# A projection moved to the token choice, and gathered rows evicted four at a time

## The chip, the cores and the metric

The kernel runs on one NeuronCore of a Trainium2 chip. Its time is the device time of one execution in microseconds (us). Five engines work side by side, each on its own list of instructions: PE (matmuls; PEld is its weight load), DVE and ACT (elementwise work), POOL (elementwise work on SBUF) and SP, which issues the DMA transfers here. A transfer is issued in the order of SP's list; an instruction that waits for a semaphore holds up what stands behind it on its engine.

## The reference

Two transformer blocks run one after the other on 512 tokens of width 1024, in float32. The first has a recurrent mixer, a cross attention and a dense feed-forward layer. The second has windowed attention beside a gated linear attention, then an expert layer and a gated embedding. The change is in the second block's end:

```python
h = h + merged @ w_out[l]
h = h + expert_choice_ffn(rmsnorm_2(h, norm_ffn[l]), w_router[l], w_exp_gate[l], w_exp_up[l], w_exp_down[l])
ple_gate = jax.nn.sigmoid(rmsnorm_2(h, norm_ple[l]) @ w_ple_gate[l])
h = h + ple_gate * (p[l] @ w_ple[l])
```

In `expert_choice_ffn` each of 16 experts takes the 64 tokens with the highest affinity to it, computes `silu(x @ gate) * (x @ up) @ down` with its own three 1024x1024 matrices, and adds the result, times the affinity, to those tokens. `p` is an input of 512 x 256 and `w_ple` one of 256 x 1024; their product depends on nothing else.

## The kernel before

**Precision.** Dense products run as three matmuls (`mm3`, L124 to L126) on operands that are split into a rounded part `hi` (ACT, L103) and a rest `lo` (DVE, L104). Expert products run in plain float32. In the trace such a float32 matmul, of an expert or of a gather, shows as two records.

**Output projection and router.** `proj_out` computes `merged @ w_out` in two halves of 512 columns; L88 loads the weights, and between the weights' split and the second half's matmuls it calls `more`, which loads expert weights. Behind each tile of the second half, `router` transposes the tile (L1263), multiplies it with the router's weights (L1269), takes the norm's factor on POOL (L188), makes a softmax and transposes the affinities on PE (L1292).

**Token choice.** DVE finds the 64 largest affinities of each expert in eight rounds (L1313, L1314), marks and numbers them (L1315, L1317). PE transposes the marks (L1323).

**Experts.** They go in eight groups g of two experts. `gather` builds a 0/1 matrix on DVE, and `rows(k)` (k = 0 to 7) picks the tokens with four matmuls into a quarter of a PSUM tile `pout`, of which there are two; ACT evicts each quarter with a scale (L1387). `hidden(e)` runs gate and up (L1478, 32 matmuls), `down(e)` the third matrix (L1503, 16 matmuls), `turned` transposes (L1493), `scatter` adds a group's result to x (L1518, L1519). In one group PE does: the first expert's hidden, the previous expert's down, the second's hidden with eight scatters, the first's down, then the gather for the next group. PE's order here is written out by hand.

**Expert weights.** The 48 matrices come as 96 pieces of 2 MB, in the order in which PE uses them: pieces 0 to 3 are expert 0's gate and up, then come, for each expert, its gate and up (4) and the previous one's down (2). So group g from 1 on uses the twelve pieces from 10 + 12(g-1). They land in a ring of eight places of 16 KB per partition: `wnext` (6), opened before the output projection, and `wlast` (2), opened when its memory is free. Pieces 6, 7 and 8 go to other tiles at first: `act_hi`, the place that `pp` gets later, and four `y4` tiles. `used` frees places and issues the next loads; a load waits until PE has finished with the piece that had the place.

**p's projection** is part of the expert loop. From group 1's end to group 2 the ring leaves three places free (`kept`). In group 2 these take p, w_ple and the split operands; in group 3 PE transposes p (L204) and multiplies (L124 to L126) into `pp`. After the experts, `pp` is multiplied with the gate.

Of the kernel before, what the change touches and what calls it, by code (L numbers as in the profile page):

```python
# [10 lines left out]
F32 = mybir.dt.float32  # L11
# [8 lines left out]
P = 128  # L20
# [15 lines left out]
def two_blocks_kernel(ctx: ExitStack, tc: tile.TileContext, A: dict, out: bass.AP, stage: int = 99):  # L36
# [751 lines left out]
    WNEXT, WLAST = 6, 2  # L788
# [38 lines left out]
    kept = [0]  # L827
# [17 lines left out]
    def used(e, m):  # L845

        free([name for _, name in pieces.pop((e, m))[::4] if name])
        load(max(0, sum(room.values()) - kept[0]))
# [6 lines left out]
    with ExitStack() as blk:  # L855
# [439 lines left out]
        side.close()  # L1295
        open_ring(late, "wnext", WNEXT, side="right")
        load(3)

        def more():
            load(WNEXT - 3)  # L1300

# [3 lines left out]
        if stage == 6:  # L1305
            return store_and_stop(x)

# [25 lines left out]
    with ExitStack() as blk:  # L1333
# [18 lines left out]
        def projected():  # L1352
            return pool.tile([P, NT, D], F32, name="pp", tag="pp", bufs=1)

        w = projected()
        homes[WNEXT + 1] = w
        homes[WNEXT + 2] = [y4() for _ in range(4)]
        load(3 + WLAST)
# [3 lines left out]
        def gather(g):  # L1362
# [17 lines left out]
            def rows(k):  # L1380
# [3 lines left out]
                for t in range(NT):  # L1384
                    PE.matmul(ps[0][:, j * P:(j + 1) * P], src[:, t, k * P:(k + 1) * P], sel[:, t, :],  # L1385
                              start=(t == 0), stop=(t == NT - 1))
                S.activation(xg[:, :, k, :], ps[0][:, j * P:(j + 1) * P].rearrange("p (e s) -> p e s", e=2), AF.Copy,  # L1387
                             scale=gcol[:, k:k + 1])
# [19 lines left out]

        def load_p():
            pr = w8((NT, 256))  # L1410
            nc.sync.dma_start(pr, A["p_2"][0, 0].rearrange("(t p) c -> p t c", p=P))
            raw = w8()
            nc.sync.dma_start(raw, A["w_ple_2"][0].rearrange("(k p) c -> p k c", p=P))
            hi, lo, pT = w8(dt=F32R), w8(dt=F32R), w8((2, 2, T), F32R)
            w8()
            return pr, raw, hi, lo, pT

        def split8(raw, hi, lo):
            S.copy(hi, raw)
            V.tensor_sub(lo, raw, hi.bitcast(F32))  # L1420
            return hi, lo

        def split_p(pr, raw, hi, lo, pT):
            split8(raw, hi, lo)
            for t in range(NT):
                transpose_split(lambda k0, n: (pT[:, 0, :, t * P:(t + 1) * P], pT[:, 1, :, t * P:(t + 1) * P]),
                                pr[:, t, :], 2)

        def project_p(pr, raw, hi, lo, pT):
            wh, wl = hi, lo  # L1430
            pp = projected()
            for t in range(NT):
# [102 lines left out]
        with tc.manual_schedule(engines={mybir.EngineType.PE}):  # L1535
            gT = None
            for g in range(NE // 2):
                a, b = 2 * g, 2 * g + 1
                if g:
# [3 lines left out]
                    if a == 6:  # L1543
                        split_p(*praw)
# [196 lines left out]
```

## Time and profile before

| | us |
|---|---|
| median of 3 runs (1952.05 to 1952.69) | 1952.14 |
| the profiled execution | 1952.34 |
| its span, first to last instruction | 1950.6 |
| PE busy | 1870.0 (96%) |
| DVE busy | 917.5 (47%) |
| ACT busy | 719.7 (37%) |
| POOL busy | 66.9 (3%) |

Of the span, the output projection ends at about 1362 us, the token choice at 1382, and the experts at about 1889. Times in the rows count from the span's start. PEclk is the granted clock of PE as a share of 2.4 GHz; 0.5 is 1.2 GHz. Durations of matmuls overlap, so what a matmul costs in a row of matmuls is read from one start to the next.

### The profile page before, as it was taken

The numbers are of one execution on the slowest core, as the hardware profiler recorded it, in microseconds if no ns is written. First come the engines' busy times: TensorE is split into PE (matmuls) and PEld (weight loads), VectorE is DVE, ScalarE is ACT, GpSimd is POOL, SyncE is SP. The second block draws the span as 40 slices with busy tenths as digits, with TensorE's granted clock in tenths as the row PEclk, the third lists the DMA queues.
The fourth block names the chain that finished last, engine by engine and source line by source line (L and its number), as shares of the span: only waits on it lengthen the run. The fifth ranks groups of instructions, "written<-read, shape, count | busy, mean of one in ns | idle before, by whom it ended". The sixth has DMA issues, their size and how long they took to land.

```text
span 1950.6 us, 24203 instructions
## 1 busy us (share of the span) xinstructions
PE 1870.0 (96%) x9723; PEld 1364.2 (70%) x9723; DVE 917.5 (47%) x1659; ACT 719.7 (37%) x1329; POOL 66.9 (3%) x103
## 2 busy tenths in 40 slices
PE   7999999999999999999999999999699989999998
PEld 6777788888888888887787778888344435434446
DVE  5777777465543444446875564453312221221146
ACT  4454774343342322325665454322121112111134
POOL 0000220000000000002000000000000000000000
PEclk9999999999999999999999999999799989999999
DMA  6222226431233333324222222336779977999951
GB/s 206 55 61 74 56 86 182 137 108 55 67 118 98 97 97 97 98 76 111 75 63 58 75 68 74 87 122 244 314 286 424 417 327 315 428 426 426 426 206 44
DMA packets 140050, 330.85 MB, mean 170 GB/s; under 512 B 9247, under 2 KB 88851, under 8 KB 127779
## 3 DMA queue, kind: packets, MB, share of 16 engines
q1 hardware_dynamic: 139522, 328.91, 46.4%
q8 instruction: 76, 1.25, 0.3%
q0 software_dynamic: 416, 0.41, 0.1%
q14 instruction: 36, 0.29, 0.0%
HBM read 327.19 MB, written 2.10 MB: 169 GB/s over the span
## 4 chain that ended last, share of the span: by engine, by line
PE 82%; DVE 7%; ACT 5%; issue 2%; DMA 1%; POOL 1%; SPq 0%; POOLq 0%; ACTq 0%; DVEq 0%
PE pd L125 16%; PE pd L124 16%; PE pd L126 16%; PE pd L1478 11%; PE pscore L1503 6%; PE pout L1385 4%; DVE lo L104 1%; ACT hi L103 1%; ACT xg L1387 1%; PE pout L1149 1%; PE pout L204 1%; POOL rs L188 1%; PE pscore L400 1%; PE pout L1046 1%; PE pscore L1119 1%
## 5 line engine op out<-in xcount | busy, mean ns | idle before, releaser
L104 DVE TENSOR_TENSOR lo<-raw,hi 128x1024 fp32r<-128x1024 f32 x208 | 253.5, 1221 | 329.5 <-ACT hi L103 326.6
L103 ACT CAST hi<-raw 128x1024 fp32r<-128x1024 f32 x208 | 218.1, 1049 | 419.6 <-PE pd L126 226.0
L124 PE MATMUL pd<-hi,act_hi 128*128 128x512 f32 (+2 forms) x584 | 227.9, 390 | 1.5 <-ACT act_hi L206 1.1
L125 PE MATMUL pd<-lo,act_hi 128*128 128x512 f32 (+2 forms) x584 | 226.6, 389 | 0.8 <-DVE lo L104 0.8
L124 PE MATMUL pd<-act_hi,hi 128*128 128x512 f32 (+1 forms) x592 | 224.2, 380 | 0.5 <-ACT act_hi L206 0.5
L126 PE MATMUL pd<-act_hi,lo 128*128 128x512 f32 (+1 forms) x592 | 224.5, 379 | 0.0
L125 PE MATMUL pd<-act_lo,hi 128*128 128x512 f32 (+1 forms) x592 | 224.2, 379 | 0.0
L1478 PE MATMUL pd<-w,xg 128*64 128x512 f32 x992 | 220.5, 600 | 0.0
L126 PE MATMUL pd<-hi,act_lo 128*128 128x512 f32 (+1 forms) x512 | 199.9, 391 | 0.0
L1478 PEld LDWEIGHTS pd<-w,xg 128*64 128x64 f32 x992 | 69.7, 138 | 135.6 <-issue 135.5
L124 PEld LDWEIGHTS pd<-hi,act_hi 128*128 128x128 f32 x584 | 110.2, 189 | 22.1 <-ACT act_hi L206 2.8
L124 PEld LDWEIGHTS pd<-act_hi,hi 128*128 128x128 f32 x592 | 111.1, 188 | 20.0 <-ACT act_hi L206 1.0
L126 PEld LDWEIGHTS pd<-act_hi,lo 128*128 128x128 f32 x592 | 111.5, 188 | 19.4 <-issue 0.2
L125 PEld LDWEIGHTS pd<-act_lo,hi 128*128 128x128 f32 x592 | 111.6, 188 | 19.1 <-DVE act_lo L207 0.4
L125 PEld LDWEIGHTS pd<-lo,act_hi 128*128 128x128 f32 x584 | 110.3, 189 | 20.2 <-DVE lo L104 1.3
L1503 PE MATMUL pscore<-w,m 128*64 128x512 f32 x496 | 109.6, 594 | 0.7 <-ACT m L1495 0.7
L126 PEld LDWEIGHTS pd<-hi,act_lo 128*128 128x128 f32 x512 | 96.6, 189 | 18.0 <-DVE act_lo L207 0.5
L253 DVE TENSOR_TENSOR x<-x,pd 128x512 f32<-128x512 f32 x83 | 55.2, 685 | 97.2 <-PE pd L126 55.9
L125 PE MATMUL pd<-lo,hh 128*128 128x512 f32 x256 | 99.7, 390 | 0.0
L124 PE MATMUL pd<-hi,hh 128*128 128x512 f32 x256 | 99.7, 389 | 0.0
L126 PE MATMUL pd<-hi,hl 128*128 128x512 f32 x256 | 99.6, 389 | 0.0
L188 POOL TENSOR_TENSOR rs<-ms,mhalf 128x1 f32<-128x1 f32 (+1 forms) x45 | 33.7, 750 | 1811.1 <-DVE ms L187 1806.9
(454 smaller groups left out, 2840.5 us busy)
## 6 DMA issues: line engine op xcount, KB each, us to landing
w<-in_w_exp_dram SPq DMA_DIRECT2D x93, 2048.0 KB, 14.0
raw<-in_w_in_dram SPq DMA_DIRECT2D x80, 512.0 KB, 3.7
raw<-in_w_up_dram SPq DMA_DIRECT2D x32, 512.0 KB, 4.2
raw<-in_w_down_dram SPq DMA_DIRECT2D x32, 512.0 KB, 3.6
raw<-in_w_xkv_dram SPq DMA_DIRECT2D x16, 512.0 KB, 5.1
raw<-in_w_out_dram SPq DMA_DIRECT2D x16, 512.0 KB, 3.8
x<-in_x_dram SPq DMA_DIRECT2D x8, 512.0 KB, 7.4
raw<-in_w_xq_dram SPq DMA_DIRECT2D x8, 512.0 KB, 3.9
```

Of the source, the lines that this page charges most:

```text
L103: S.copy(hi[:, :size], raw[:, :size])
L104: V.tensor_sub(lo[:, :size], raw[:, :size], hi[:, :size].bitcast(F32))
L124: PE.matmul(ps, ah, bh, start=first, stop=False)
L125: PE.matmul(ps, ah, bl, start=False, stop=False)
L126: PE.matmul(ps, al, bh, start=False, stop=last)
L188: G.tensor_tensor(rs[:, :n], ms[:, :n], mhalf[:, :n], op=OP.pow)
L204: PE.transpose(ps[:, k, :], src[:, (k0 + k) * P:(k0 + k + 1) * P], ident)
L253: return lambda t, ps: V.tensor_add(x[:, t, c:c + 512], x[:, t, c:c + 512], ps)
L400: PE.matmul(ps[H * hf:H * hf + H, t, :].rearrange("p (n two b) -> p two n b", two=2, b=B), km[:, o:o + H], qv, start=True, stop=True)
L1385: PE.matmul(ps[0][:, j * P:(j + 1) * P], src[:, t, k * P:(k + 1) * P], sel[:, t, :], start=(t == 0), stop=(t == NT - 1))
L1478: PE.matmul(ps[64 * half:64 * half + 64, :], xg[:, e % 2, k, :], w[:, 512 * half:512 * half + 512], start=(k == 0), stop=(k == KT - 1))
L1503: PE.matmul(py[64 * half:64 * half + 64, :], h[:, k % 4, 64 * (k // 4):64 * (k // 4) + 64], w[:, 512 * half:512 * half + 512], start=(k == ...
```

## The change

p's projection moves from the expert loop to the output projection and the token choice. `more` loads p and both halves of w_ple and transposes p; after `proj_out`, the second half of w_ple is split by ACT and POOL, and the 48 matmuls follow into a tile `pp` of its own. The ring keeps eight places, five in `wnext` and three in `wlast`, since `pp` takes one from the memory ahead; piece 5 goes to `act_hi` and 6 to the `y4` tiles, and no piece to `pp`'s place. The rule that kept three places free goes. In `rows`, DVE evicts four quarters at once.

```diff
-    WNEXT, WLAST = 6, 2
+    WNEXT, WLAST = 5, 3
...
-        load(max(0, sum(room.values()) - kept[0]))
+        load(sum(room.values()))
...
+        pp = late.enter_context(tc.tile_pool(name="pp", bufs=1, side="right")).tile([P, NT, D], F32, name="pp")
         open_ring(late, "wnext", WNEXT, side="right")
         load(3)
...
         def more():
+            pr = grow_tile().rearrange("p (t c) -> p t c", t=NT)
+            nc.sync.dma_start(pr, A["p_2"][0, 0].rearrange("(t p) c -> p t c", p=P))
+            wple.append(chunk_b(w_ple, 0, 0))
+            load_ahead(w_ple, 0, 512)
             load(WNEXT - 3)
+            for t in range(NT):
+                transpose_split(lambda k0, n: (pT[:, 0, :, t * P:(t + 1) * P], pT[:, 1, :, t * P:(t + 1) * P]),
+                                pr[:, t, :], 2)
...
+        raw = loaded.pop((w_ple.tensor.name, w_ple.offset, 0, 512))
+        hi, lo = [pools["w"].tile([P, WC], F32R, name=n) for n in ("hi", "lo")]
+        S.copy(hi, raw)
+        G.tensor_sub(lo, raw, hi.bitcast(F32))
+        wple.append([w.rearrange("p (a b) -> p a b", a=2) for w in (hi, lo)])
+        for n in range(2):
+            wh, wl = wple[n]
+            for t in range(NT):
+                ts = slice(t * P, (t + 1) * P)
+                ps = pd()
+                for k in range(2):
+                    mm3(ps, pT[:, 0, k, ts], pT[:, 1, k, ts], wh[:, k, :], wl[:, k, :], k == 0, k == 1)
+                S.copy(pp[:, t, 512 * n:512 * n + 512], ps)
...
-        homes[WNEXT + 1] = w
-        homes[WNEXT + 2] = [y4() for _ in range(4)]
-        load(3 + WLAST)
+        homes[WNEXT + 1] = [y4() for _ in range(4)]
+        load(2 + WLAST)
...
-                S.activation(xg[:, :, k, :], ps[0][:, j * P:(j + 1) * P].rearrange("p (e s) -> p e s", e=2), AF.Copy,
-                             scale=gcol[:, k:k + 1])
+                if j == 3:
+                    V.tensor_mul(xg[:, :, k - 3:k + 1, :].rearrange("p e k s -> p k e s"),
+                                 ps[0].rearrange("p (k e s) -> p k e s", k=4, e=2),
+                                 gcol[:, k - 3:k + 1, None, None].to_broadcast([P, 4, 2, CAP]))
...
-                    if a == 6:
-                        split_p(*praw)
...
-                if a == 4:
-                    kept[0] = 0
-                    praw = load_p()
-                    pheld = held[-3:]
...
-                if a == 6:
-                    pp = project_p(*praw)
-                    free(pheld)
...
-                if a == 2:
-                    kept[0] = 3
```

PE's list at the end of the output projection, before: the last tile's second half is transposed (L1263) and routed (L1269), the affinities are transposed (L1292), and the next row already belongs to the token choice.

```order
L126 MATMUL pd<-hi,u_10578 128x256
L1263 MATMUL pout<-ident,x 128x128 x4
L1269 MATMUL pscore<-wr,grow 128x16 x4
L1292 MATMUL pscore<-ident,aff 16x128
L1323 MATMUL pscore<-ident,raw 128x16 x8
L1385 MATMUL pout<-m_11194,x 128x128 x16
```

The same place now (`pT` is p transposed and split):

```order
L1262 MATMUL pout<-ident,x 128x128 x2
L124 MATMUL pd<-hi,pT 128x512
L125 MATMUL pd<-lo,pT 128x512
L1262 MATMUL pout<-ident,x 128x128 x2
L1268 MATMUL pscore<-wr,grow 128x16 x2
L126 MATMUL pd<-hi,pT 128x512
L124 MATMUL pd<-hi,pT 128x512
L125 MATMUL pd<-lo,pT 128x512
L126 MATMUL pd<-hi,pT 128x512
L1268 MATMUL pscore<-wr,grow 128x16 x2
L124 MATMUL pd<-hi,pT 128x512
L125 MATMUL pd<-lo,pT 128x512
```

The 48 matmuls of the projection stand between the router's last transpositions: 14 ahead of the last L1291 (L1292 before), the other 34 behind it and ahead of L1348 (L1323 before).

SP's list at the loads of pieces 6, 7 and 8, before, with the semaphores that each row waits for (`y` is a `y4` tile):

```order
L841 DMA act_hi<-in_w_exp_dram 128x4096 [waits DMAHW2_49,PE_49]
L841 DMA pp<-in_w_exp_dram 128x4096 [waits DMAHW3_49,DMAHW6_49,DVE_49,PE_49]
L839 DMA y_11177<-in_w_exp_dram 128x1024 [waits DMAHW4_49]
L839 DMA y_11178<-in_w_exp_dram 128x1024 [waits DMAHW5_49]
L839 DMA y_11179<-in_w_exp_dram 128x1024
L839 DMA y_11180<-in_w_exp_dram 128x1024 [waits DMAHW7_49]
```

The same place now, from piece 5 to piece 8:

```order
L840 DMA act_hi<-in_w_exp_dram 128x4096 [waits DMAHW4_49,PE_49]
L838 DMA y_11281<-in_w_exp_dram 128x1024 [waits DMAHW5_49,DMAHW2_49,Pool_49]
L838 DMA y_11282<-in_w_exp_dram 128x1024 [waits DVE_49,PE_49]
L838 DMA y_11283<-in_w_exp_dram 128x1024 [waits DMAHW7_49,PE_49]
L838 DMA y_11284<-in_w_exp_dram 128x1024 [waits DMAHW0_49]
L840 DMA w_11290<-in_w_exp_dram 128x4096 [waits DMAHW1_49]
L840 DMA w_11292<-in_w_exp_dram 128x4096 [waits DVE_49]
```

The `y4` tiles now lie where the split w_ple lies: the first quarter waits for POOL's subtraction, the second for a matmul of the projection's first half (n = 0), the third for the projection's last matmul. Pieces 7, 8 and 9 stand behind them.

## Rows read from the trace of the kernel before

**Rows 1.** The page: busy time of the engines, and the transfers' rate in the 40 slices.

```profile
PE 1870.0 (96%) x9723; PEld 1364.2 (70%) x9723; DVE 917.5 (47%) x1659; ACT 719.7 (37%) x1329; POOL 66.9 (3%) x103
...
GB/s 206 55 61 74 56 86 182 137 108 55 67 118 98 97 97 97 98 76 111 75 63 58 75 68 74 87 122 244 314 286 424 417 327 315 428 426 426 426 206 44
```

**Rows 2.** The waits of PE from 1340 us to the end: who waited for whom, us in total, times, longest.

```profile
PE pout L1385 <- ACT xg L1387: 22.0, 48, 0.5
PE pscore L1323 <- DVE raw L1315: 12.5, 1, 12.5
PE pout L204 <- DVE w L207: 5.2, 1, 5.2
```

**Rows 3.** PE's timeline of one gather, that for group 2, and the first expert behind it: start, us, engine, line, operation, out<-in, records, and the idle time before with its releaser.

```profile
1493.95 1.16 PE L1385 MATMUL pout<-oh,act_hi 128*128 128x128 f32 x8
1495.57 1.16 PE L1385 MATMUL pout<-oh,act_hi 128*128 128x128 f32 x8 [0.46 <-ACT xg L1387]
...
1498.80 2.05 PE L1385 MATMUL pout<-oh,act_hi 128*128 128x128 f32 x16 [0.46 <-ACT xg L1387]
1501.31 1.16 PE L1385 MATMUL pout<-oh,act_hi 128*128 128x128 f32 x8 [0.46 <-ACT xg L1387]
...
1505.54 0.96 PE L1393 MATMUL pscore<-aff,oh 128*128 128x16 f32 x8
...
1506.91 13.95 PE L1478 MATMUL pd<-w,xg 128*64 128x512 f32 x64
```

**Rows 4.** PE's timeline: the starts of the first expert of groups 1, 3 and 4 (that of group 2 is in rows 3).

```profile
1447.04 13.95 PE L1478 MATMUL pd<-w,xg 128*64 128x512 f32 x64
...
1566.79 13.95 PE L1478 MATMUL pd<-w,xg 128*64 128x512 f32 x64
...
1647.66 13.95 PE L1478 MATMUL pd<-w,xg 128*64 128x512 f32 x64
```

**Rows 5.** Stretches behind the first gather and in the expert stage: from:to, length, then busy us (and records) of PE, PEld, DVE, ACT and POOL, PE's clock, the transfers' share of 16 engines and GB/s.

```profile
1395.00:1400.00 5.00, 3.62 (x28) 3.05 (x27) 0.00 (x0) 1.10 (x3) 0.00 (x0) 1.00 0.85 305
...
1660.00:1860.00 200.00, 191.75 (x972) 85.83 (x970) 39.46 (x68) 30.28 (x67) 0.00 (x0) 1.00 1.01 427
```

**Rows 6.** PE's timeline in group 3: p's transpositions and what follows them, and the first of the 48 matmuls of p's projection with what follows the last.

```profile
1588.03 0.38 PE L204 MATMUL pout<-ident,w 128*128 128x128 f32 x2
...
1594.59 1.11 PE L204 MATMUL pout<-ident,w 128*128 128x128 f32 x4 [5.15 <-DVE w L207]
1595.63 9.63 PE L1478 MATMUL pd<-w,xg 128*64 128x512 f32 x32
...
1636.16 0.48 PE L124 MATMUL pd<-w,w 128*128 128x512 f32 x1
...
1647.13 0.60 PE L1493 MATMUL pout<-ident,m 128*128 128x128 f32 x4
```

**Rows 7.** The timeline from the output projection's end to the first gather: PE's rows and POOL's one.

```profile
1362.53 0.38 PE L1263 MATMUL pout<-ident,x 128*128 128x128 f32 x2
...
1364.65 0.55 POOL L188 TENSOR_TENSOR rs<-ms,mhalf 128x1 f32<-128x1 f32 x1 [6.73 <-DVE ms L187]
...
1366.84 0.38 PE L1292 MATMUL pscore<-ident,aff 128*16 128x128 f32 x1 [1.78 <-DVE aff L1291]
1379.68 0.60 PE L1323 MATMUL pscore<-ident,raw 16*128 16x16 f32 x4 [12.45 <-DVE raw L1315]
...
1382.54 2.14 PE L1385 MATMUL pout<-m,x 128*128 128x128 f32 x8 [0.96 <-DVE m L1370]
...
1391.08 3.65 PE L1478 MATMUL pd<-w,xg 128*64 128x512 f32 x16
1394.66 1.16 PE L1385 MATMUL pout<-m,x 128*128 128x128 f32 x8
```

**Rows 8.** Groups of instructions by line and shape, from 1400 us on: line, engine, operation, out<-in, shapes, count, busy us, mean ns of one, idle time before.

```profile
L253 DVE TENSOR_TENSOR x<-x,pd 128x512 f32<-128x512 f32 x28 | 18.0, 685 | 41.1 <-PE pd L1519 41.1
...
L1439 ACT COPY pp<-pd 128x512 f32<-128x512 f32 x8 | 4.7, 589 | 6.2 <-PE pd L126 6.2
```

**Rows 9.** PE's timeline of the last group.

```profile
1827.29 13.95 PE L1478 MATMUL pd<-w,xg 128*64 128x512 f32 x64
...
1867.18 7.09 PE L1503 MATMUL pscore<-w,m 128*64 128x512 f32 x32
1874.20 1.10 PE L1532 MATMUL pout<-ident,x 128*128 128x128 f32 x8
...
1881.34 7.09 PE L1503 MATMUL pscore<-w,m 128*64 128x512 f32 x32 [0.68 <-ACT m L1495]
```

**Rows 10.** Stretches as in rows 5, from the output projection's end to the first gather.

```profile
1350.00:1360.00 10.00, 10.00 (x69) 8.85 (x68) 2.84 (x13) 2.48 (x8) 1.11 (x2) 1.00 0.00 2
...
1365.00:1370.00 5.00, 0.44 (x2) 0.09 (x1) 3.59 (x11) 0.49 (x2) 0.20 (x1) 0.53 0.97 411
...
1385.00:1390.00 5.00, 3.95 (x17) 3.47 (x17) 0.00 (x0) 0.82 (x3) 0.00 (x0) 0.58 0.83 351
```

**Rows 11.** The one line of POOL subtractions of some size: times, ns of one (shortest, median, longest), first and last start, shapes.

```profile
L532 POOL TENSOR_TENSOR t<-t,t x8: 1265/1381/1820, 203.3 to 273.1; 128x512 fp32r<-128x512 f32 x8
```

**Rows 12.** SP's timeline behind group 1's first matmul.

```profile
1450.73 0.33 SPq L841 DMA_DIRECT2D w<-in_w_exp_dram  x1
```

**Rows 13.** The view of the expert weights as a tile: time from a transfer's issue to its landing, over all pieces.

```profile
DMA to landing us min/median/max: 8.7/14.1/24.2
```

More of the change, by code (lines that the diff above doesn't have):

```diff
@@ L826, in two_blocks_kernel @@
     room = {"wnext": WNEXT, "wlast": WLAST}
-    kept = [0]
     def load(n):
@@ L1295, in two_blocks_kernel @@
         side.close()
+        pp = late.enter_context(tc.tile_pool(name="pp", bufs=1, side="right")).tile([P, NT, D], F32, name="pp")
         open_ring(late, "wnext", WNEXT, side="right")
         load(3)
+        pj = blk.enter_context(tc.tile_pool(name="pj", bufs=1))
+        pT = pj.tile([P, 2, 2, T], F32R, name="pT")
+        w_ple = A["w_ple_2"][0]
+        wple = []
         def more():
+            pr = grow_tile().rearrange("p (t c) -> p t c", t=NT)
+            nc.sync.dma_start(pr, A["p_2"][0, 0].rearrange("(t p) c -> p t c", p=P))
+            wple.append(chunk_b(w_ple, 0, 0))
+            load_ahead(w_ple, 0, 512)
             load(WNEXT - 3)
+            for t in range(NT):
+                transpose_split(lambda k0, n: (pT[:, 0, :, t * P:(t + 1) * P], pT[:, 1, :, t * P:(t + 1) * P]),
+                                pr[:, t, :], 2)
         proj_out(lambda k, t: (mh[:, t, k, :], ml[k // 2][:, k % 2, t * P:(t + 1) * P]),
@@ L1350, in two_blocks_kernel @@
         homes[WNEXT] = w
-        def projected():
-            return pool.tile([P, NT, D], F32, name="pp", tag="pp", bufs=1)
-        w = projected()
-        homes[WNEXT + 1] = w
-        homes[WNEXT + 2] = [y4() for _ in range(4)]
-        load(3 + WLAST)
+        homes[WNEXT + 1] = [y4() for _ in range(4)]
+        load(2 + WLAST)
         affs = small.tile([P, NE], F32, name="affs")
@@ L1407, in gather @@
             return xg, rows, affinities, back
[L1409 to L1432, printed above, removed]
-                ts = slice(t * P, (t + 1) * P)
-                for n in range(2):
-                    ps = pd()
-                    for k in range(2):
-                        mm3(ps, pT[:, 0, k, ts], pT[:, 1, k, ts], wh[:, k, 512 * n:512 * n + 512],
-                            wl[:, k, 512 * n:512 * n + 512], k == 0, k == 1)
-                    S.copy(pp[:, t, 512 * n:512 * n + 512], ps)
-            return pp
         def load_gate(k):
```

## The prediction, made before the changed kernel ran

> **What bounds the kernel now.** I read the page first: PE is busy 96% of the span, and in the last third of the slices the transfers run at some 426 GB/s for long stretches, far above what they do before [rows 1]. Then PE's own waits from 1340 us on [rows 2]. Three lines hold nearly all of them: 48 waits of 0.46 us, 22.0 in all, for ACT's evictions of the gathered rows (L1385 for L1387); 12.5 us for DVE's choice of the tokens; 5.2 us for a split of p. PE therefore sets the end in the expert stage, and the reader is to look for what PE does there besides experts. The timeline of one gather shows the pattern: four matmuls (8 records) begin every 1.62 us, but the one place where the accumulator changes (x16) puts the second four only 0.89 us behind the first [rows 3]. The starts of the first expert of each group give the period: 59.87 us (1506.91 - 1447.04), and 80.87 for the group that also does p's work [rows 3, 4].
>
> The transfers come second, and closely. One piece is 2,097,152 bytes; at the 427 GB/s that 200 us of the expert stage show it takes 4.91 us [rows 5], and a group needs 12 of them: 58.9 us against PE's 59.9. So PE can be made only 1 us faster per group before the transfers bind, unless they have a lead. They have one, since the eight places fill while PE gathers.
>
> **Term 1, p's work leaves the loop: -21.0 us.** The third group starts at 1566.79 and ends at 1647.66, 80.87 later; 80.87 - 59.87 = 21.0 [rows 4]. Its parts agree: 7.6 us from 1588.03 to 1595.63, most of it waits; 2.5 us because the next 32 matmuls took 9.63 instead of 7.09 after those waits; 11.0 us from 1636.16 to 1647.13 [rows 6, 9].
>
> **Where it goes.** The 48 matmuls take 11.0 us, 0.229 each, from the first one's start to what follows the last [rows 6]. In PE's new order 14 of them stand ahead of the last transposition of the affinities and 34 behind it. PE waited there anyway: 1.78 us before that transposition and 12.45 before L1323 [rows 7]. Of the 14 the last eight stand directly ahead of it: 8 x 0.229 = 1.8 us, as long as the wait. The six others (1.4 us) stand from 1362.53 on between steps of the router, which take the same turns between PE, ACT and DVE as before; I count 0 for them and up to 1.4 as the bound, if PE had no gap there. The 34 (7.8 us) end at about 1376, and DVE delivers its first result at 1379.6. So some 4 us of cover remain; a projection longer than that would delay the choice one for one, as would those 1.4 us. ACT's eight evictions (0.59 each, [rows 8]) have four accumulators ahead of them.
>
> The preparation is new work in the output projection, where PE is full: eight transpositions, 1.10 us as the eight of L1532 [rows 9]. I take **+1.0**, between 0.9 and 2.5 if their two accumulators make PE wait. The splits of p are evictions of ACT and DVE, about 0.6 or 0.7 each like those of [rows 8], eight in all; ACT and DVE are busy 2.5 and 2.8 of 10 us there [rows 10]: hidden. On SP, p and half of w_ple stand in front of the fourth piece and the other half in front of the fifth; the transfers do nothing from 1350 to 1360 [rows 10], so that costs nothing. POOL's subtraction of 128x1024 has no row; the nearest, 128x512, takes 1.27 to 1.82 [rows 11], so 1.3 to 3.6, I take 2.8. It stands ahead of the last tile's L188 in POOL's queue, and the token choice waits for that one. Its input is ready near 1361.4, so it ends near 1364.2, before L188 started (1364.65, [rows 7]): 0, at worst +0.4, and nothing to win.
>
> **Term 2, the evictions: -30.1 us.** With one accumulator for four pieces and no reader in between, PE issues 32 matmuls in a row. Six of the eight steps fall from 1.62 to 0.89: 6 x 0.72 = 4.3 us a group (0.72 rather than 0.73 for rounding), and 7 groups: 30.1. The DVE eviction is put at 0.69 us, as the 128x512 addition from PSUM (L253); it could cost from 0.4 to 1.2, since its output is strided, and either way it is hidden: the affinities and transpositions that follow take PE 1.4 us, and DVE is busy 39.5 of 200 us [rows 3, 5, 8].
>
> **Term 3, the first gather: -2.2 and -0.4 us.** The second half (L1385 at 1394.66 and after) loses three such waits: -2.2 [rows 7]. The first half runs while the clock stands at 0.5, from about 1365.3 to 1389.2: between 0.5 and 1, 0.53 in one stretch of 5 us puts the fall 0.3 us behind its start, and 0.58 in another the rise 0.8 us ahead of its end [rows 10]. It becomes denser, but its first expert must now wait for a whole eviction, some 0.95 us, where before it started at once (1391.08). If the clock does what it did: 28 records by 1389.2 at 0.235, four more at 0.11, the eviction, start at 1390.65: -0.4. PE is idle for some 4 us before it (1376 to 1379.7), and in the loop, behind a wait of 5.15 us, 32 matmuls took 9.63 us instead of 7.09 [rows 6]; so I expect the fall again.
>
> **Term 4, the transfers: +3.8 us.** Piece 6's place and part of the ring lie in the memory of the projection's operands, and SP issues in its order: piece 6's third quarter waits for the last projection matmul, with 7, 8 and 9 behind it. So transfers that ran at 411 GB/s and later at 351 there [rows 10] now stop from about 1370 to 1376. PE needs piece 7 only near 1420, and it lands near 1387: nothing is lost there. What matters is the ring. Group g uses pieces 10+12(g-1) on; piece 18 takes the place of piece 10, and was issued at 1450.73, 3.7 us after the group's first matmul [rows 4, 12]. Call that first matmul's time H. A lone transfer lands 8.7 us after its issue at the least, 3.8 more than 4.91 [rows 13], so piece n lands at H + 3.7 + 3.8 + 4.91(n-17). With terms 1 and 2 PE's groups take 55.6, so it starts group 7 at H + 333.5 and piece 93, 43.4 later (1867.18 + 3.5 - 1827.29, [rows 9]), at H + 376.9. Piece 93 lands at H + 380.7. **+3.8**, all in the last two groups; later pieces are not late. If that overhead is 3.0 and a piece takes 4.90, it is +2.2; at 417 GB/s, the lowest full slice [rows 1], a piece takes 5.03 and it is +12.9. I take the 200 us row.
>
> The row says 427 GB/s from HBM for 200 us. A page of the Trainium skill, "DMA: Bandwidth & Descriptors", section "Where 436 GB/s comes from", says otherwise: about 358 GB/s of HBM per core bind such transfers, and 435 is only the fabric's ceiling. By 358 a piece would take 5.86 us and a group 70.3, the stage would already be bound by transfers, and term 2 would bring nothing. The trace disagrees with the first figure and comes close to the second.
>
> **The sum.** -21.0 - 30.1 - 2.2 - 0.4 + 1.0 + 3.8 = -48.9. Against the profiled execution (1952.34; its span is 1950.6, 1.7 less) that is **1903.4 us**; the median of the runs shown, 1952.14, is 0.2 lower, which changes nothing here. Nothing measurable means within 0.2%, or 3.9 us.
>
> **Rivals.**
> - *The clock stays up through the choice of tokens.* For it: the idle stretch shrinks from 12.45 us to some 4. Against: the 5.15 us wait [rows 6]. Then the first half takes 4 x 0.89 from 1382.54, plus 0.95: 1387.05 instead of 1390.65, so 3.6 less: **1899.8**.
> - *The transfers bind from the third group on.* For it: a margin of 1 us a group, and 417 GB/s in one full slice. Against: 427 over 200 us. 76 pieces at 0.12 us more: **1912.5**.
> - *The evictions are not what PE waits for.* If PE waits at each step for something else, terms 2 and 3's first part go, and so does the wait for transfers: 1903.4 + 32.3 - 3.8 = **1931.9**. Against: the x16 step, and the order, in which the 32 matmuls now stand in one row.
> - *Slower: transfers one at a time.* If places come free singly, each transfer runs alone. In 1395 to 1400, where one did, 305 GB/s at a share of 0.85 make 359 [rows 5], 5.84 us a piece. Piece 95 lands at H + 7.5 + 78 x 5.84 = H + 463.0; H is 1447.04 + 1.0 - 0.4 - 2.2 - 4.3 = 1441.1, so 1904.1. Its matmuls began at 1881.34 + 3.5 = 1884.8 before [rows 9], so the end moves by +19.3: **1971.6**. It is slower than before once a piece takes over 5.59 us (375 GB/s). Against: whenever PE waits for transfers all free places are already queued, and then they overlap.
>
> **Chances.** Forecast 0.62 (its own range 1899 to 1909: 2.2 instead of 3.8, up to 1.5 more for the transpositions or the 14 matmuls, up to 4 more if PE's waits in the last group halve the clock again). Clock stays 0.17; transfers bind 0.13; evictions not the cause 0.05; slower 0.03. The range takes in the first three: from 1896.0 (the clock's case without any wait for transfers) to 1916 (the second rival with 1.5 for the transpositions and 2 of the clock's 4); 0.96 faster, 0.01 the same, 0.03 slower.
>
> **What will show it.** In the changed profile: no ACT releaser on L1405 and gathers of some 7.2 us; groups 55.6 us apart until group 5; p's matmuls between 1363 and 1377 with the token choice no later than now; PE waits named after DMAs, a few us in groups 6 and 7 alone. I am wrong if the groups stay above 58 us, if the waits for DMAs exceed 8 us in all, or if the first L1313 comes more than 2 us later.

## The result, and the profile after

The changed kernel takes 1905.8 us (median of 4 runs, 1905.32 to 1906.05) where the one before took 1952.1: a ratio of 0.976, 95% interval 0.9745 to 0.9779. The forecast was 1903.4, so the gain of 46.3 us came out 2.4 smaller than forecast. The profiled execution has a span of 1904.2 us, 46.4 less than before.

The page first, the same parts as [rows 1]:

```profile
PE 1856.3 (97%) x9723; PEld 1360.2 (71%) x9723; DVE 926.9 (49%) x1675; ACT 695.7 (37%) x1266; POOL 69.1 (4%) x104
...
GB/s 210 56 56 72 68 68 180 146 117 61 56 118 93 100 100 93 95 78 100 100 66 58 71 74 56 89 88 188 205 378 374 427 428 425 426 428 427 426 305 45
```

PE was busy for 13.7 us less, and its idle time fell by 32.7 (46.4 - 13.7): most of what went was waiting. PE's waits from 1330 us on, where [rows 2] had 22.0, 12.5 and 5.2:

```profile
PE pscore L1348 <- DVE raw L1340: 4.7, 1, 4.7
PE pd L1467 <- DMA w<-in_w_exp_dram: 3.7, 5, 1.3
PE pout L1521 <- ACT w L1522: 1.1, 3, 0.7
PE pout L1405 <- DVE m L1390: 1.0, 1, 1.0
...
PE pscore L1291 <- DVE aff L1290: 0.5, 1, 0.5
```

The 48 waits for ACT are gone, the wait for the choice fell from 12.45 to 4.7, and there is a new kind: 3.7 us for transfers of expert weights. PE's timeline of the gather for group 1 and the first expert behind it answers to [rows 3]:

```profile
1433.79 7.41 PE L1405 MATMUL pout<-oh,act_hi 128*128 128x128 f32 x64
1441.04 0.96 PE L1415 MATMUL pscore<-aff,oh 128*128 128x16 f32 x8
```

All 64 records stand in one piece and take 7.25 us up to the affinities; one eviction by DVE (L1408) takes 0.69 us. The starts of the first expert of groups 1, 6 and 7 from PE's timeline, as in [rows 4]:

```profile
1442.41 13.95 PE L1467 MATMUL pd<-w,xg 128*64 128x512 f32 x64
...
1720.08 13.95 PE L1467 MATMUL pd<-w,xg 128*64 128x512 f32 x64
...
1777.59 13.95 PE L1467 MATMUL pd<-w,xg 128*64 128x512 f32 x64
```

Five groups take 277.67 us, 55.53 each; group 6 takes 57.51. In group 7 the waits for transfers stand in PE's timeline:

```profile
1799.70 3.65 PE L1467 MATMUL pd<-w,xg 128*64 128x512 f32 x16 [0.66 <-DMA w<-in_w_exp_dram]
1804.62 3.65 PE L1467 MATMUL pd<-w,xg 128*64 128x512 f32 x16 [1.26 <-DMA w<-in_w_exp_dram]
```

The end of the output projection and the token choice in PE's timeline, as in [rows 7]:

```profile
1365.10 0.38 PE L1262 MATMUL pout<-ident,x 128*128 128x128 f32 x2
...
1377.41 0.39 PE L126 MATMUL pd<-hi,pT 128*128 128x512 f32 x1
1382.52 0.60 PE L1348 MATMUL pscore<-ident,raw 16*128 16x16 f32 x4 [4.72 <-DVE raw L1340]
...
1385.38 6.83 PE L1405 MATMUL pout<-m,x 128*128 128x128 f32 x32 [0.95 <-DVE m L1390]
1393.05 3.65 PE L1467 MATMUL pd<-w,xg 128*64 128x512 f32 x16 [0.83 <-issue]
```

The projection leaves PE idle for 4.7 us, close to the 4 or so of the forecast, but all of it stands later than before: the last turn of x at 1365.10 instead of 1362.53. PE's clock in stretches from there (columns as in [rows 5]):

```profile
1378.00:1380.00 2.00, 0.00 (x0) 0.00 (x0) 1.90 (x6) 0.42 (x1) 0.00 (x0) 1.00 0.51 84
1380.00:1382.00 2.00, 0.00 (x0) 0.00 (x0) 1.93 (x4) 0.00 (x0) 0.00 (x0) 0.85 0.93 358
1382.00:1384.00 2.00, 0.75 (x6) 0.67 (x7) 1.64 (x3) 0.21 (x1) 0.00 (x0) 0.50 1.16 483
...
1390.00:1392.00 2.00, 2.00 (x13) 2.00 (x11) 0.00 (x0) 0.00 (x0) 0.00 (x0) 0.59 0.96 410
```

It is at 1.0 (2.4 GHz) while PE works on the projection and falls to 0.5 (1.2 GHz) while PE waits behind it: 0.85 in the stretch from 1380 to 1382 puts the fall near 1381.4. The 0.59 of the last row puts the rise near 1391.6. Before, it was low for 24 us; now for 10. This differs from one execution to the next: in the runs below whose matmuls are the same up to there (e3, e6 to e9, e11, e12) it is low for 7 to 10 us, and the 32 records of the first gather's first half take 5.75 to 6.52 us instead of the 6.83 above.

**A yardstick for the experiments.** The start of the last four attention transpositions (L1234 before, L1233 after), which no edit touches, wanders between 1311.5 and 1314.8 us from one execution to the next. So runs are also compared by the time from there to the end of the span: 638.5 us before (1950.6 - 1312.14), 591.2 in the changed kernel (1904.2 - 1313.03), and 590.4 when it was run again (e11). The kernel before, timed beside the experiments, had medians from 1953.3 to 1954.6 us instead of 1952.1, so a difference of 1 or 2 us between times of different experiments says little.

### The profile page after: what moved, and what is told of

Same layout as the page of the kernel before. It is cut to its first block, busy times and chain, and to the rows that moved or that the text cites. A ratio compares the mean times of both kernels' runs of the same rounds, so it can differ in the third digit from the quotient of the medians.

```text
span 1904.2 us, 24167 instructions
## 1 busy us (share of the span) xinstructions
PE 1856.3 (97%) x9723; PEld 1360.2 (71%) x9723; DVE 926.9 (49%) x1675; ACT 695.7 (37%) x1266; POOL 69.1 (4%) x104
## 4 chain that ended last, share of the span: by engine, by line
PE 79%; DVE 8%; DMA 6%; ACT 4%; issue 2%; POOL 1%; SPq 0%; POOLq 0%; ACTq 0%; DVEq 0%
PE pd L125 16%; PE pd L126 16%; PE pd L124 16%; PE pd L1467 10%; PE pscore L1492 5%; DMA w<-in_w_exp_dram 3%; PE pout L1405 3%; DVE lo L104 2%; ACT hi L103 1%; PE pout L1148 1%; PE pout L204 1%; POOL rs L188 1%; PE pscore L400 1%; PE pout L1045 1%; PE pscore L1118 1%
## 5 line engine op out<-in xcount | busy, mean ns | idle before, releaser
L1492 PE MATMUL pscore<-w,m 128*64 128x512 f32 x512 | 113.5, 594 | 1.1 <-ACT m L1484 0.9
L188 POOL TENSOR_TENSOR rs<-ms,mhalf 128x1 f32<-128x1 f32 (+1 forms) x45 | 33.6, 748 | 1758.8 <-DVE ms L187 1753.0
```

The costliest lines, as they stand in the source:

```text
L188: G.tensor_tensor(rs[:, :n], ms[:, :n], mhalf[:, :n], op=OP.pow)
L1492: PE.matmul(py[64 * half:64 * half + 64, :], h[:, k % 4, 64 * (k // 4):64 * (k // 4) + 64], w[:, 512 * half:512 * half + 512], start=(k == ...
```

## The experiments

**e1: the evictions alone.** In the kernel before:

```diff
-                S.activation(xg[:, :, k, :], ps[0][:, j * P:(j + 1) * P].rearrange("p (e s) -> p e s", e=2), AF.Copy,
-                             scale=gcol[:, k:k + 1])
+                if j == 3:
+                    V.tensor_mul(xg[:, :, k - 3:k + 1, :].rearrange("p e k s -> p k e s"),
+                                 ps[0].rearrange("p (k e s) -> p k e s", k=4, e=2),
+                                 gcol[:, k - 3:k + 1, None, None].to_broadcast([P, 4, 2, CAP]))
```

> The kernel before with the eviction of four pieces by DVE as its only edit; p stays in the loop. Theory (each wait of 0.46 us for ACT costs 0.72 us, and transfers bind only once their lead is used up): gathers of groups 1 to 7 shorten by 4.34 us each (30.4), the first gather by 2.1 and 0.4; the group with p's work lets the transfers catch up, so PE waits for no transfer: 1952.1 - 32.9 = 1919.2 us, groups of 55.5 us and one of 76.5. Rival (transfers bind every group at 58.9 us): groups gain 1.0 instead of 4.34, so some 1943. Rival (the wait is not the eviction's): 1952.

Measured: 1918.1 us, ratio 0.982 (0.9808 to 0.9835). Groups take 55.53 us, the one with p's work 75.08 instead of the 76.5 expected, and the gathers look like those of the changed kernel:

```profile
1485.38 7.41 PE L1385 MATMUL pout<-oh,act_hi 128*128 128x128 f32 x64
1494.00 13.95 PE L1480 MATMUL pd<-w,xg 128*64 128x512 f32 x64
```

The theory holds. Two things were off. PE does wait once for a transfer in the last group, 0.9 us. And p's group is 19.55 us longer than the others, not 21.0: behind the same wait of 5.15 us the next 32 matmuls take 8.13 us here and took 9.63 before [rows 6], since the clock is back at 1.0 some 2.1 us after they begin instead of 5.2. So 1.5 of the 21.0 us of term 1 depend on how long the clock is low there.

**e2: p's projection alone.** The changed kernel with ACT's line put back.

> The changed kernel with ACT's eviction of single pieces put back; p's work stays at the token choice. Theory: groups take 59.87 us, longer than the 58.9 us of twelve transfers, so the waits for transfers (5.3 us in the changed kernel) go; p's work out of the loop is worth 21.0, its preparation costs 1.7, the choice comes 0.3 later, and the first gather gains about 1 from a clock that is low for a shorter time: 1952.1 - 20.0 = 1932 us, within 2. The two edits' gains then do not add up: 32.9 + 20.0 against the 46.3 of both, and the difference is the waits for transfers. Rival (gains add up, the waits named after transfers have another cause): 1905.8 + 32.9 = 1938.7.

Measured: 1935.5 us, 0.991 (0.9896 to 0.9923). All seven periods are 59.87 us, and from 1400 to 1780 us PE waits for ACT and for no transfer:

```profile
PE pout L1405 <- ACT xg L1407: 17.9, 39, 0.5
PE pscore L1490 <- ACT m L1482: 0.2, 1, 0.2
```

So the waits for transfers belong to the shorter groups, as the theory says. Its sum was 3.5 us too low. Of this, 2.9 are the first gather: from its first matmul to the expert behind its affinities it took 1.9 us longer than before, instead of 1 us less, since the low clock now falls on the gather and the first expert's matmuls, where before part of it fell on an idle PE (16 records of the first expert take 4.44 us instead of 3.65). By the yardstick e1 gains 35.1 us, e2 17.4, both 47.3: 5.2 are missing. That is as much as the changed kernel loses to transfers (below), but e1 holds 1 us of waits too and the first gathers differ, so the match is not exact.

**e3: fewer bytes.** Experts 10 to 15 take gate's pieces for up, 12 pieces are never loaded.

```diff
-    order = [(e, m, q) for e, m in order for q in range(KT // 4)]
+    order = [(e, m, q) for e, m in order for q in range(KT // 4) if e < 10 or m != 1]
...
-                    w = pieces[e, m][k][0]
+                    w = pieces[e, 0 if e >= 10 else m][k][0]
```

> The changed kernel, where experts 10 to 15 use their gate matrices for up as well, so that 12 of the 96 pieces are not transferred; the matmuls stay the same. Part of the computation is changed by this. Theory (5.3 us in groups 6 and 7 are waits for transfers): these go, groups 6 and 7 take 55.5 us like the others, and the time is 1905.8 - 5.3 = 1900.5 us. Rival (PE loses those 5.3 us to something else, such as its clock after short waits): no change, 1905.8.

Measured: 1901.0 us, 0.973 (0.9719 to 0.9746). Group 6, in PE's timeline:

```profile
1718.14 13.95 PE L1467 MATMUL pd<-w,xg 128*64 128x512 f32 x64
1765.05 7.41 PE L1405 MATMUL pout<-oh,act_hi 128*128 128x128 f32 x64
1773.67 13.95 PE L1467 MATMUL pd<-w,xg 128*64 128x512 f32 x64
```

Group 6 takes 55.53 us again. From group 7's start to the last expert's second half PE needs 54.06 us, as it did before the change (1881.34 - 1827.29 = 54.05, [rows 9]); the changed kernel needed 57.36. So the waits for transfers cost 2.0 us in group 6 and 3.3 in group 7, 5.3 in all, more than the 3.7 that the waits' view adds up. Of this 1.4 came back here as a new wait for DVE's last split of y (L1503, 1.5 us).

**e4: p's transpositions later**, behind the output projection's last matmul.

```diff
-            for t in range(NT):
-                transpose_split(lambda k0, n: (pT[:, 0, :, t * P:(t + 1) * P], pT[:, 1, :, t * P:(t + 1) * P]),
-                                pr[:, t, :], 2)
...
         raw = loaded.pop((w_ple.tensor.name, w_ple.offset, 0, 512))
+        for t in range(NT):
+            transpose_split(lambda k0, n: (pT[:, 0, :, t * P:(t + 1) * P], pT[:, 1, :, t * P:(t + 1) * P]),
+                            prs[0][:, t, :], 2)
```

> The changed kernel with p's eight transpositions moved behind the output projection's last matmul, into the stretch of the token choice. Theory (the preparation costs PE 1.7 us because PE is full there, and PE waits 4.7 us for the choice): the output projection ends 1.7 us earlier, the 1.7 us are taken out of the wait of 4.7, and the time is 1904.1. Rival (what stands ahead of the last transposition of the affinities delays the choice one for one): the first selection of the largest affinities is late by 1.1 us or more against the end of the output projection, and the gain is under 0.6: 1905.2 to 1905.8.

Measured: 1903.6 us, 0.975 (0.9732 to 0.9759). From the attention's last transpositions to the last turn of x it takes 50.4 us (1362.98 - 1312.55), as before the change, instead of 52.1: the 1.7 us are gone there. The choice is 0.2 later against that turn, and PE's wait for it is shorter by what moved in:

```profile
1380.60 0.42 PE L1350 MATMUL pscore<-ident,raw 16*128 16x16 f32 x4 [3.08 <-DVE raw L1342]
```

So the rival's reason falls: the last transposition of the affinities comes 4.5 us behind that turn, 4.7 in the changed kernel. Its size does not: group 6 now takes 58.28 us, and by the yardstick only 0.2 to 1.0 us is left (590.2 against 591.2 and 590.4).

**e5: PE kept busy** behind the projection.

```diff
+        ps = pd()
+        for i in range(22):
+            PE.matmul(ps, pT[:, 0, 0, :P], wple[0][0][:, 0, :], start=True, stop=True)
```

> The changed kernel with 22 more matmuls of 128x512 behind p's projection, whose result nobody reads; they take some 5.0 us, as long as PE's wait of 4.7 us for the choice. Theory (the first gather is slow because PE's clock falls to 0.5 after PE has stood idle): the clock stays at 1.0, the first 32 matmuls of the gather take 3.7 us instead of 6.83, and the time is 1905.8 - 3.1 = 1902.7 us. Rival (the clock falls there whatever PE does just before, or the added matmuls delay the transpositions behind them by as much): 1905.8 or more.

Measured: 1905.2 us, 0.975 (0.9735 to 0.9761). First PE's timeline, then the stretches with PE's clock (columns as in [rows 5]):

```profile
1377.83 5.15 PE L1334 MATMUL pd<-hi,pT 128*128 128x512 f32 x22
...
1385.40 5.31 PE L1408 MATMUL pout<-m,x 128*128 128x128 f32 x32 [0.96 <-DVE m L1393]
```

```profile
1384.00:1386.00 2.00, 0.99 (x7) 0.92 (x7) 1.41 (x7) 0.00 (x0) 0.00 (x0) 0.76 0.75 197
1386.00:1388.00 2.00, 2.00 (x11) 2.00 (x11) 1.49 (x8) 0.00 (x0) 0.00 (x0) 0.50 1.03 401
1388.00:1390.00 2.00, 2.00 (x18) 2.00 (x18) 0.00 (x0) 0.00 (x0) 0.00 (x0) 0.88 1.08 414
```

The clock falls later, at about 1385, and is low for some 3.4 us instead of 7 to 10: behind the added matmuls PE still has gaps of 0.7 and 1.0 us between the transpositions of the choice and the gather. The 32 records take 5.31 us, 1.5 less than in the changed kernel's first profile, but only 0.6 less than in its second (e11):

```profile
1384.01 5.92 PE L1405 MATMUL pout<-m,x 128*128 128x128 f32 x32 [0.95 <-DVE m L1390]
```

So the gather gains half or less of what the theory gave it, and group 6 takes 58.43 us, so that by the yardstick (590.4) nothing certain is left. The direction of the theory holds; that filling one wait would hold the clock does not.

**e6: two accumulators in turn**, evicted by ACT piece by piece.

```diff
-                j = k % 4
-                if j == 0:
-                    ps[0] = pout()
+                j = k // 2 % 2 if g == 0 else k // 2
+                if k == 0 or g == 0 and k == 4:
+                    ps[:] = [pout(), pout()]
...
-                    PE.matmul(ps[0][:, j * P:(j + 1) * P], src[:, t, k * P:(k + 1) * P], sel[:, t, :],
+                    PE.matmul(ps[k % 2][:, j * P:(j + 1) * P], src[:, t, k * P:(k + 1) * P], sel[:, t, :],
...
-                if j == 3:
-                    V.tensor_mul(xg[:, :, k - 3:k + 1, :].rearrange("p e k s -> p k e s"),
-                                 ps[0].rearrange("p (k e s) -> p k e s", k=4, e=2),
-                                 gcol[:, k - 3:k + 1, None, None].to_broadcast([P, 4, 2, CAP]))
+                S.activation(xg[:, :, k, :], ps[k % 2][:, j * P:(j + 1) * P].rearrange("p (e s) -> p e s", e=2), AF.Copy,
+                             scale=gcol[:, k:k + 1])
```

> The changed kernel with ACT evicting single pieces again, but with the pieces going to two accumulators in turn, so that one is read while the other is written. Theory (PE waited because the eviction and the next matmuls shared an accumulator, not because ACT is slow or evicts singly): PE's waits for ACT go as they did with DVE's eviction of four, gathers of groups 1 to 7 take some 7.4 us for their 64 records, and the time is 1905.8 us, within 1.5. Rival (a single eviction by ACT, 0.37 us and its signal both ways, takes longer than the 0.9 us of the four matmuls beside it): each piece still takes 1.0 to 1.6 us, 1911 to 1935 us.

Measured: 1905.3 us, 0.975 (0.9737 to 0.9767). PE's timeline of the gather for group 1:

```profile
1431.96 7.52 PE L1405 MATMUL pout<-oh,act_hi 128*128 128x128 f32 x64
1439.32 0.96 PE L1413 MATMUL pscore<-aff,oh 128*128 128x16 f32 x8
```

7.36 us instead of 7.25, and no wait for ACT. So neither DVE nor the batch of four was needed: what cost 0.72 us at each step was that the piece being evicted and the piece being computed shared an accumulator. No run shows whether that wait could be left out of the program. Single pieces help the first gather: its first expert follows without the wait of 0.83 us for a whole eviction.

**e7: half places.** The same memory as sixteen places of 8 KB, 192 loads.

```diff
-    WNEXT, WLAST = 5, 3
+    WNEXT, WLAST = 10, 6
...
-    order = [(e, m, q) for e, m in order for q in range(KT // 4)]
+    order = [(e, m, q) for e, m in order for q in range(KT // 2)]
...
-            wv = A["w_exp"][e, m, q]
+            wv = A["w_exp"][e, m, q // 2][:, 2 * (q % 2):2 * (q % 2) + 2, :]
```

> The changed kernel with sixteen places of 8 KB per partition instead of eight of 16 KB, and 192 transfers of 1 MB instead of 96 of 2 MB, in the same order. Theory (the waits for transfers in groups 6 and 7 come from the lead that the ring gives at a group's start: a place is freed only when all its matmuls are done): places come free 1.7 us earlier and a half lands sooner than a whole, so of some 5 us of waits 1 to 2 are left: 1902 us. Rival (twice as many transfers of half the size run at a lower rate): at 1% less each group of twelve pieces takes 0.6 us more, the waits begin earlier, and the time is 1910 us or more.

Measured: 1909.3 us, 0.977 (0.9756 to 0.9783): the rival. From 1450 to 1660 us neither kernel waits for a transfer. The stretch in the changed kernel, columns as in [rows 5], and then here:

```profile
1450.00:1660.00 210.00, 210.00 (x1094) 95.60 (x1091) 49.93 (x87) 23.57 (x47) 0.00 (x0) 1.00 1.01 427
```

```profile
1450.00:1660.00 210.00, 210.00 (x1102) 96.64 (x1099) 49.73 (x86) 23.39 (x46) 0.00 (x0) 1.00 1.01 420
```

The rate falls from 427 to 420 GB/s. A piece of 2 MB then takes 0.08 us longer, 6.2 us over 76 pieces, which is more than the 1.7 us of earlier places; from group 1's start to the end this run takes 4.4 us longer than the changed kernel.

**e8: another home for piece 6.** `homes[WNEXT + 1]` becomes `homes[WNEXT + 3]` for the y4 tiles.

> The changed kernel with the four y4 tiles as the place of piece 8 instead of piece 6; pieces 6 and 7 go to the last ring's places, so that SP can issue two pieces before it reaches the loads that wait for the projection's last matmul. Theory (the transfers' pause from 1375 to 1380 us costs nothing, since PE needs piece 7 only near 1420 and the lead at group 1's start is set by when places come free): 1905.8 us, within the noise. Rival (the pause takes lead away, which is what PE waits for in groups 6 and 7): up to 5 us of transfers are won, 1901 to 1903.

Measured: 1905.9 us, 0.975 (0.9738 to 0.9765). Nothing changed, as expected, though the pause from 1375 to 1380 stayed too (82 GB/s instead of 70): pieces 6 and 7 go out at 1377.44, only behind the projection's last matmul (1377.20). So the edit itself shows little of what an earlier transfer would be worth. The stretches behind group 1's start show it, in the changed kernel (group 1 at 1442.41) and then here (1441.89):

```profile
1444.00:1446.00 2.00, 2.00 (x12) 0.68 (x10) 0.00 (x0) 0.00 (x0) 0.00 (x0) 1.00 0.00 0
```

```profile
1444.00:1446.00 2.00, 2.00 (x12) 0.72 (x10) 0.00 (x0) 0.00 (x0) 0.00 (x0) 1.00 0.00 0
```

The transfers stand still: all pieces up to 17 have landed, and piece 18 goes out only 3.7 us behind group 1's start, when its place is free. What the choice does to earlier transfers is used up by then, so the rival falls.

**e9: two queues.** ACT issues every second piece.

```diff
+                q_ = nc.scalar if i >= 18 and i % 2 else nc.sync
-                nc.sync.dma_start(w.rearrange("p a b -> p (a b)"), wv.rearrange("p a b -> p (a b)"))
+                q_.dma_start(w.rearrange("p a b -> p (a b)"), wv.rearrange("p a b -> p (a b)"))
```

> The changed kernel with every second expert piece from piece 19 on issued by ACT instead of SP, so that two queues feed the transfers. Theory (the 16 engines that carry a transfer are the limit at some 4.94 us a piece, not the gaps between transfers of one queue): the rate stays at 427 GB/s and the time at 1905.8 us, within 1. Rival (one queue leaves gaps between transfers): the rate rises by 1% or more, the waits of some 5 us in groups 6 and 7 shrink to 1 or less, 1900.5 to 1902. Second rival (two transfers side by side share the engines, so that each lands up to one piece later, or ACT is held up by its waits for places): 1908 to 1911.

Measured: 1913.9 us, 0.979 (0.978 to 0.9807), slower than the changed kernel and above the second rival's range. The stretch of e7's rows reads 422 GB/s here, PE's waits from 1340 us on:

```profile
PE pd L1468 <- DMA w<-in_w_exp_dram: 8.1, 6, 2.0
...
PE pscore L1493 <- DMA w<-in_w_exp_dram: 1.4, 5, 0.4
```

But two queues do not move less: from 1480 to 1660 the rate is 427 GB/s, as with one (426), at a share of 1.01 in both. So the 16 engines were full with one queue, and the first rival falls. What the 422 holds is one gap, at whose end ACT's second and third load go out:

```profile
1460.00:1465.00 5.00, 5.00 (x26) 1.77 (x24) 0.74 (x1) 1.27 (x2) 0.00 (x0) 1.00 0.66 220
```

```profile
1448.73 14.46 ACTq L841 DMA_DIRECT2D w<-in_w_exp_dram  x3
```

Up to 18 us behind group 1's start (1441.51) three loads have gone out, where the changed kernel issued five: loads were held up on both queues, where the second rival named ACT's. At 220 GB/s instead of 427, 5 us cost some 2.4 us of transfers. How much of the rest is the later landing of two transfers side by side was not separated.

**e10: the parts that helped, together.** e4's move; matmuls without a reader in three gaps of PE; ACT with two accumulators in group 0 alone.

```diff
+        def warm(n):
+            ps = pd()
+            for _ in range(n):
+                PE.matmul(ps[:, :P], ident, ident, start=True, stop=True)
+
+        warm(13)
...
+            warm(3 if dst is chosen else 4)
```

> The changed kernel with three edits: p's transpositions behind the output projection's last matmul, as in the run that tried that alone; 20 matmuls of 128x128 without a reader in PE's waits for the token choice (13, 3 and 4), on operands that no transfer waits for; and in the first gather ACT's eviction of single pieces from two accumulators in turn, DVE's eviction of four from then on. Theory (before group 1 PE loses 1.7 us to the transpositions, 3.1 to a clock of 0.5 and 0.8 to the whole eviction ahead of the first expert, and the transfers' lead is counted from group 1's start, so that what is won before it stays won): group 1 starts 73.4 us after the last turn of x instead of 77.3, that turn comes 1.7 earlier against the attention's last step, and the time is 1905.8 - 5.5 = 1900.3 us. Rival (what is won ahead of group 1 is given back as longer waits for transfers in groups 6 and 7, since these then set the end): 1903.5 to 1905.

**e11: the changed kernel again**, on the same chip.

> The changed kernel itself once more, beside the two runs sent with it, so that they are compared on the same chip: 1905.8 us, within 1.5. The theory and its rivals say nothing different of it; it shows how far the waits for transfers in groups 6 and 7 vary from one execution to the next (3.7 us in the first profile), and how far the start of the output projection does.

Measured: e10 1901.7 us, 0.973 (0.972 to 0.9747), its runs 1900.65 to 1903.56; e11 1905.3 us, 0.975 (0.9736 to 0.9763), its runs 1903.85 to 1905.42. The runs don't overlap: e10 is 3.6 us faster than the changed kernel beside it, and 52.9 faster than the kernel before on that chip (1954.5). In its timeline PE has hardly a gap through the choice:

```profile
1379.57 3.06 PE L1338 MATMUL pd<-ident 128*128 128x128 f32 x26
1382.81 0.42 PE L1356 MATMUL pscore<-ident,raw 16*128 16x16 f32 x4 [0.17 <-DVE raw L1348]
1383.16 0.94 PE L1338 MATMUL pd<-ident 128*128 128x128 f32 x6
...
1385.49 4.50 PE L1414 MATMUL pout<-m,x 128*128 128x128 f32 x32
1389.93 3.65 PE L1479 MATMUL pd<-w,xg 128*64 128x512 f32 x16
```

All its stretches of 5 us from 1375 to 1395 have a clock of 1.0. From the attention's last transpositions to group 1 it needs 124.4 us, where the changed kernel needed 129.4 and, in e11, 128.4: 4.0 to 5.0 of the 5.5 expected. Of it 0.6 to 0.9 came back in group 6, as the rival says, but no more: 58.36 us, where the changed kernel took 57.51 and 57.74. e4, e5 and e8 show the same (58.2 to 58.4). What makes the transfers late there against group 1's start was not found. It is not the issue: piece 18 goes out 3.7 us and piece 53 158.1 us behind group 1's start in all of these, but piece 53 lands after 184.1 and 184.3 us in the changed kernel's two profiles and after 184.8 to 185.0 in the four runs. Nor is it the rate, 427 GB/s from 1450 to 1660 us in each.

**e12: one place less.** The edit turned out not to do this.

```diff
-        load(sum(room.values()))
+        load(max(0, sum(room.values()) - (e < 14)))
```

> The changed kernel where the ring keeps one of its eight places free until the matrices of expert 14 are used, so that transfers run one piece less ahead of PE. Theory (the waits in groups 6 and 7 are the lead at group 1's start, less what each group wears off it: a group takes PE 55.5 us and the transfers twelve times 4.94): the lead is one piece or 4.9 us shorter, every piece from 18 on lands 4.9 us later against group 1's start, PE first waits some one and a half groups earlier, and the time is 1905.5 + 4.9 = 1910.4 us. Rival (the transfers' end is set by their number and rate alone, from the token choice on, not by how many places there are): 1905.5. Second rival (with one place less the transfers pause at every gather, where PE frees no place for 8.6 us): some us in each of seven groups, 1915 or more.

Measured: 1905.1 us, 0.976 (0.9738 to 0.9771), and group 6 takes 57.50 us. It looks like the first rival, but the edit did not shorten the lead: SP's timeline has piece 18 issued at

```profile
1443.63 0.33 SPq L840 DMA_DIRECT2D w<-in_w_exp_dram  x1
```

which is 3.7 us behind this run's group 1 (1439.93), as in the changed kernel (1446.11 against 1442.41). `load` only sets where a load stands in SP's list; each load still takes the place eight before it and goes out when that comes free. How the lead depends on the number of places stays untested.

## Why the prediction was right

The time, 1905.8, lies in the forecast's own range of 1899 to 1909. Step by step, by differences of starts in the two profiles:

| term | forecast | measured |
|---|---|---|
| 1: p's work out of the loop | -21.0 | -21.0 |
| p's transpositions | +1.0 | +1.7 |
| p's matmuls ahead of the choice | 0 | +0.3 |
| 2: evictions, groups 1 to 7 | -30.1 | -30.5 |
| 3: first gather, second half | -2.2 | -2.1 |
| 3: first gather, first half | -0.4 | -0.9 |
| 4: waits for transfers | +3.8 | +5.3 |
| ahead of the output projection | 0 | +0.9 |

- **Term 1** held to the tenth; e2 shows seven equal periods without it. Part of the agreement is built in, since both columns take the 21.0 from the trace of the kernel before. In e1 p's group takes only 19.55 us more than the others: with the evictions already changed, this term would have been 1.5 smaller.
- **Term 2** held, and e1 shows it alone; DVE's eviction took the 0.69 us forecast, inside the bounds of 0.4 to 1.2 for its strided output. The forecast's rival "the evictions are not what PE waits for" falls. The forecast's reason was stated too narrowly: e6 shows that ACT does as well from two accumulators.
- **The preparation** was mis-sized. Eight transpositions cost about 1.0 us where they stand; the remaining 0.7 appears later, between 1349 and 1356, where PE's order around the router differs; 0.5 of it is a wait for a tile's affinities (L1291 for DVE's L1290) that the kernel before does not have, and not the two accumulators that the forecast's bound was built on. e4 has no such wait and shows that all 1.7 go with the move. The bound of 2.5 held.
- **POOL's subtraction** took 2.38 us (forecast 2.8) and ended at 1366.47, ahead of L188's input (1367.08): no cost, as forecast.
- **The choice**: the 14 matmuls cost 0.3, not 0. The first selection came 2.83 us later than before, beyond the 2 us that I had named as a sign of being wrong; 0.9 of it was there before the output projection began and 1.7 is the preparation. That 0.9, a line of the table, is no cost of the change: the start that it is taken from wanders by 3.3 us between executions.
- **The clock** fell, as the forecast said against its rival, and the first gather took the form forecast for it. It was low for 10 us instead of 24: PE worked until 1377.8, and the fall came behind that. The first half's -0.9 is one execution; the other runs with the same gather (e3, e7 to e9, e11, e12) have -1.2 to -1.95.
- **Term 4** had the right mechanism and place (groups 6 and 7, and only because groups became shorter: e2, e3), but its size was short by 1.5. The time of a piece was taken too low: piece 53 lands 184.1 and piece 93 381.8 us behind group 1's start, 4.94 us a piece instead of 4.91, so piece 93 came 1.1 us later than forecast (380.7). The overhead of 3.8 us fits, though [rows 13] holds the landings of 13 of the 99 loads only: by it piece 53 was due at 184.3. Why a piece takes that much longer was not found, since the rate between these two landings reads 427 GB/s as well. Of the other 0.4 some 0.3 lie on PE's side: with groups of 55.53 us instead of 55.6 it wanted piece 93 that much earlier. The rival in which transfers bind from the third group on falls with five groups of 55.53 us; the one at 359 GB/s falls with 427. The Trainium skill's figure of some 358 GB/s of HBM per core ("DMA: Bandwidth & Descriptors", section "Where 436 GB/s comes from") did not bind here either: 427 for 210 us. The same page, in its section "Measured", gives about 358 for each of two cores that stream from one HBM domain at once; this kernel runs on one core, and no run here shows two.

The sum of the measured column is -46.3, against -46.4 of the spans. Without the wandering 0.9 the misses are +2.6 (preparation, matmuls, second half, transfers) and -0.9 (evictions, first half), so that the sum came out closer than its parts, which is luck.

## What to carry to other kernels

Here every wait of PE in a row was as long as the last, one step, where the accumulator changes, was short, and the shared accumulator was the cause; so look for such a step. A second accumulator in turn was worth as much as a batched eviction by another engine (e6). Before an engine's waits are taken out, work out what the next resource needs in the same period: here 59.9 us against 58.9 decided that 5 of some 51 us would come back as waits for transfers, two groups before the end. Work that was moved into PE's wait for another engine cost 0.3 us itself and 1.7 for its preparation, which stood where PE was full; so look at the preparation too. Moving it took the 1.7 us away there (e4), though 0.2 to 1.0 of it reached the end.

## What was not expected

Transfers of 1 MB ran at 420 GB/s where those of 2 MB ran at 427 (e7). Two queues ran at the same 427 as one but for one gap, and the kernel still lost 8.6 us against the changed kernel beside it (e9). PE's clock fell in e5 although PE had worked up to its first transposition; it stayed at 1.0 only where the gaps behind were filled as well (e10, which also moved p's transpositions into the wait, so that the gaps alone were not tested).
